# Cache tiles' outputs copied from input to output in memory instead of stored from SBUF

## The chip, the cores and the metric

The kernel runs on one core of a Trainium2 chip. The metric is the device time of one execution in microseconds. The engines named below are TensorE (PE; PEld is its weight load), VectorE (DVE), ScalarE (ACT), GpSimd (POOL) and SyncE (SP), which here issues nearly all of the DMA transfers. SBUF is the core's working memory, PSUM the memory that TensorE accumulates in; "memory" in this document is the chip's main memory, where inputs and outputs lie.

## The reference, cut to what matters

One layer of a decoder is computed for a prompt of 256 positions and for 8 sample sequences of 4 new positions each, all with the same weights. Besides the two activations the layer returns the caches of keys and values after the step. For the sample sequences that is the old cache with the new rows behind it:

```python
for g, (win, dil) in enumerate(GROUPS):
    kg, vg = k[:, :, g], v[:, :, g]
    ...
        kg = jnp.concatenate([kv_prev[g][:, :, 0].astype(x.dtype), kg], axis=1)
        vg = jnp.concatenate([kv_prev[g][:, :, 1].astype(x.dtype), vg], axis=1)
        o, l = _dilated_band_sample(q[:, :, g], kg, vg, slopes[g], dil)
    keep = min(win, kg.shape[1])
    kv_new.append(jnp.stack([kg[:, kg.shape[1] - keep:], vg[:, vg.shape[1] - keep:]], axis=2))
```

So the old rows of the three cache groups (windows 128, 512 and 2048) have to reach the outputs unchanged, and a part of them is also read by the attention of the sample sequences. In the third group, with its dilation of 16, attention reads 4 of 16 classes of rows; the other 12, called the rest, are only passed on. The rest of the layer is one input projection, a gated short convolution (mixer A), the attention (mixer B), two branch projections, an output projection, a layer norm, a feed-forward part with its own short convolution, and a second layer norm.

## The kernel before, in words

The host lays the arrays out by block. Weights lie as blocks of 128 x 2048 numbers (1 MB), one for each product. The part of the old cache that attention reads lies as 18 tiles of keys (`ck`) and 18 tiles of values (`cv`), 1 MB each: tiles 0 and 1 belong to the first group, 2 to 9 to the second, 10 to 17 to the third. The rest of the third group lies as 48 blocks of 1 MB (`rest`). The same layout holds for the outputs `o_ck`, `o_cv` and `o_rest`.

The kernel is a chain of 300 products on TensorE. Each multiplies one weight block with the 288 tokens in three passes of 16 matmuls (lines 222 to 224), for which a weight is split into a high part `whi` (by ScalarE) and a low part `wlo` (by VectorE), both in line 228, half a block at a time. The loaded block lies in `wst`, of which there are three buffers; `whi` and `wlo` have four buffers of half a block. `product` calls `prepare`, which issues the load of a later block on SP's queue (line 183), and then lets the steps of the sample attention run that are due (`sample_steps`). The order of the products is: queries, keys and values, then mixer A (48 products), gates and branch A in turns (32), gates and branch B in turns (32, branch B with blocks of 0.25 MB), the output projection (16), and three rounds of up and down projections.

The sample attention is a list of events with due times counted in products. A tile of the cache is loaded five products ahead of its work (`cache_load`, line 426, in one of three buffers `cache`), stored to its output three products ahead (`cache_store`, line 430), and then worked on. Tiles 0 and 1 are read by matmuls (line 476). All others are multiplied in place by queries or by attention weights: half of each half-tile by ScalarE (line 441), half by VectorE (line 445), and then summed by VectorE (line 447). Key tiles stand 2.75 products apart (`TILE_K`), value tiles 2.5 (`TILE_V`). A scheduler at build time puts the instructions of each engine in one order, by its own estimate of when each can run. The build also sets the waits, among them that of lines 441 and 445 for the store that reads the same tile, and that of the store for the load.

The rest of the third group goes from input to output in memory by `copy_rest` (line 147), one block behind every weight load number n with n above 116 and n modulo 11 equal to 0, 4 or 8 (line 187), which begins where branch B does. `behind` fixes an order on a queue without a wait. All of these transfers, weights, cache tiles, stores and copies, are issued by SP.

Of the kernel before, what the change touches and what calls it, by code (L numbers as in the profile page):

```python
# [20 lines left out]
KD = D // P  # L21
# [47 lines left out]
NB_QKV = 3 * NG * NH  # L69
N_CT = 18  # L70
N_REST = 48
# [22 lines left out]
def layer_kernel(ctx: ExitStack, tc: tile.TileContext, ins, outs):  # L94
    nc = tc.nc
    pe, dve, act, pool, sp = nc.tensor, nc.vector, nc.scalar, nc.gpsimd, nc.sync
# [12 lines left out]
    def sb(pl, shape, tag, dt=F32, bufs=None):  # L109
        return pl.tile(shape, dt, tag=tag, name=nm(tag), bufs=bufs)  # L110
# [22 lines left out]
    w_load = [None]  # L133
    steps_on = [False]
    n_product = [2]
    rest = [0]
    no_sync = mybir.DependencyInfo(mybir.DependencyClass.NoSync, mybir.DependencyReason.DATA)

    def behind(i, after):

        tc.add_manual_dep(i.ins, after.ins.name, no_sync, reason="pace")

    def copy_rest(after):
        if rest[0] < N_REST:
            n = rest[0]
            rest[0] += 1
            behind(sp.dma_start(outs["o_rest"][n], ins["rest"][n]), after)


    w_split = []  # L150
# [1 line left out]
    def half_block(st, k0, n):  # L152
        hi = sb(wp, [P, HK, P], "whi", F32R, bufs=4)
        lo = sb(wp, [P, HK, P], "wlo", F32R, bufs=4)
        w_split[:] = split(hi[:, :n, :], lo[:, :n, :], st[:, k0 : k0 + n, :])
        return hi, lo, n
# [21 lines left out]
    def prepare():  # L178
        src, nk = next(w_left, (None, 0))
        if nk == 0:  # L180
            return
        st = sb(wp, [P, KD, P], "wst")
        d = sp.dma_start(st[:, :nk, :], src.rearrange("p (k c) -> p k c", c=P))  # L183
        loads[0] += 1
        n = loads[0]
        w_load[0] = d
        if n > NB_QKV + 5 * KD and n % 11 in (0, 4, 8):
            copy_rest(d)
        w_ready.append([half_block(st, k0, min(HK, nk - k0)) for k0 in range(0, nk, HK)])

# [12 lines left out]
    def product(x):  # L203

        w = w_ready.pop(0)
        if not w_ready:
            prepare()
        n_product[0] += 1
        if steps_on[0]:
            next(steps, None)  # L210
        o = acc(x[0].shape[-1])
        mms(o, w, x)
        prompt_step()
        return o.rearrange("p a h -> p h a")
# [59 lines left out]
    def first_three():  # L274

        prepare()
        o = [acc() for _ in range(3)]

        def first_w(lo, b, k):
            if b < 2:  # L280
                return w_two_lo[k // HK][:, b, k % HK] if lo else w_two_hi[:, b, k]
            return (w_one_lo if lo else w_one_hi)[k // HK][:, k % HK]

        before = None
        for k0, n, _ in FIRST:
            for term in range(3):
                for k in range(k0, k0 + n):
                    xk = x[term == 1][:, k].rearrange("p h a -> p a h")
                    for b in range(3):
                        i = pe.matmul(  # L290
                            o[b], first_w(term == 2, b, k), xk, start=k == 0 and term == 0, stop=k == KD - 1 and term == 2
                        )
                        if before is not None:
                            behind(i, before)
                        before = i
        return [t.rearrange("p a h -> p h a") for t in o]
# [125 lines left out]
    cache_tiles = {}  # L422
# [3 lines left out]
        behind(sp.dma_start(t, ins[which][n]), w_load[0])  # L426
        cache_tiles[which, n] = t

    def cache_store(which, n):
        sp.dma_start(outs["o_" + which][n], cache_tiles[which, n])  # L430

    def weighted(which, n, half, w):

        c, (g, b) = cache_tiles[which, n], divmod(n - 2, NB)
        cols = NT * P
        for j in (2 * half, 2 * half + 1):
            e = c[:, j * cols : (j + 1) * cols]
            if j % 2 == 0:
                for t in range(NT):
                    e_t = e[:, t * P : (t + 1) * P]  # L440
                    act.activation(e_t, e_t, AF.Copy, scale=w[:, g + 1, j, b * NT + t : b * NT + t + 1])  # L441
            else:
                e3 = e.rearrange("p (t k) -> p t k", t=NT)
                w3 = w[:, g + 1, j, b * NT : (b + 1) * NT].unsqueeze(2).broadcast_to([P, NT, P])
                dve.tensor_tensor(e3, e3, w3, ALU.mult)  # L445
        j = slice(2 * half, 2 * half + 2)
        dve.tensor_reduce(  # L447
            parts[:, g, :, j, b * NT : (b + 1) * NT].rearrange("p k j t -> p j t k"),
            c[:, 2 * half * cols : (2 * half + 2) * cols].rearrange("p (j t k c) -> p j t k c", j=2, t=NT, c=SQ),
            AX.X, ALU.add, apply_transpose=True,  # L450
        )

    def sample_events():
# [98 lines left out]
        for which, w, first, apart in (("ck", q_s, SCORES_AT, TILE_K), ("cv", sT_w, VALUES_AT, TILE_V)):  # L552
            for n in range(N_CT):
                at = first + n if n < 2 else first + 2 + (n - 2) * apart
                yield at - 5, partial(cache_load, which, n)
                yield at - 3, partial(cache_store, which, n)
                if n < 2:
                    yield at - 1, partial(masks, n, w)
                    yield at, partial(first_group, which, n)
                else:  # L560
                    for half in range(2):
                        yield at + half * apart / 2, partial(weighted, which, n, half, w)

    events = sorted(sample_events(), key=lambda e: e[0])

    def sample_steps():
# [496 lines left out]
```

## Time and profile before

| | |
|---|---|
| median of 3 runs | 1748.38 us (1745.45 to 1749.07) |
| the profiled execution | 1746.45 us |
| its span, first to last instruction | 1744.7 us |
| mean granted TensorE clock | 0.995 |
| TensorE busy | 1717.8 us, 98% |
| VectorE, ScalarE, GpSimd busy | 1102.0, 866.2, 260.9 us |
| moved by DMA | 436.15 MB |
| read from memory, written to it | 389.78 MB, 94.53 MB |

A row of a group of instructions has its line, engine, operation, output and inputs by the program's names, shapes, count, busy time and mean duration. A row of waits has who waited, for whom, the sum in us, how often, and the longest. A row of DMA issues has the median time from issue to landing. In the rows of stretches each engine's busy time is followed by its number of instructions. A matmul's recorded end is modelled, and matmuls overlap, so that a busy TensorE need not be one at its full pace.

### The profile page before, as it was taken

To read this page: it belongs to the slowest core of one execution; us is meant where nothing else is said; L and a number is where in the kernel's file an instruction comes from. 1 tells how busy PE (TensorE), PEld (TensorE's weight loads), DVE (VectorE), ACT (ScalarE), POOL (GpSimd) and SP (SyncE) were. 2 spreads that over 40 slices of the span, in tenths; PEclk is the share of its full clock that TensorE was granted. 3 is DMA by queue.
4 is the path that set the end of the run, shared out by engine and by line. 5 is a ranking of instruction groups with operands and counts; after the bars stand their busy time and mean duration, and the time that the engine had idled before them with its cause. 6 is when DMAs were issued, how large, how long until landed. Compare 5 with 4: busy or idle time off the path is not lost.

```text
span 1744.7 us, 33546 instructions
## 1 busy us (share of the span) xinstructions
PE 1717.8 (98%) x14034; PEld 1710.6 (98%) x14034; DVE 1102.0 (63%) x1406; ACT 866.2 (50%) x1398; POOL 260.9 (15%) x404
## 2 busy tenths in 40 slices
PE   9999999999999999999999999999999999999996
PEld 9999999999999999999999999999999999999996
DVE  5566567666877664455688888865555554555554
ACT  5455465444556443344445655544445443344444
POOL 0000001100010000011264332300111100011165
PEclk9999999999999999999999999999999999999998
DMA  9886777877887874567766655656666565656662
GB/s 334 316 329 262 298 274 264 313 285 293 299 314 303 323 266 169 181 241 265 268 230 229 229 220 230 229 219 237 221 228 232 220 237 219 231 227 222 223 221 99
DMA packets 61496, 436.15 MB, mean 250 GB/s; under 512 B 7456, under 2 KB 9504, under 8 KB 17440
## 3 DMA queue, kind: packets, MB, share of 16 engines
q1 hardware_dynamic: 59616, 429.29, 65.6%
q10 hardware_dynamic: 1728, 4.72, 0.7%
q8 instruction: 109, 1.79, 0.4%
q14 instruction: 43, 0.35, 0.1%
HBM read 389.78 MB, written 94.53 MB: 278 GB/s over the span
## 4 chain that ended last, share of the span: by engine, by line
PE 78%; DMA 14%; DVE 3%; issue 2%; ACT 2%; SPq 0%; ACTq 0%; DVEq 0%; POOL 0%; POOLq 0%
PE acc L222 26%; PE acc L224 26%; PE acc L223 26%; DMA cache<-in_cv 4%; DMA cache<-in_ck 4%; DMA out_o_ck<-cache 4%; DMA out_o_cv<-cache 2%; DVE wlo L228 2%; ACT cache L441 1%; PE acc L290 1%; DVE sw L447 1%; DMA dd<-in_w_in 0%; SPq L183 0%; ACT whi L228 0%; ACT yah L789 0%
## 5 line engine op out<-in xcount | busy, mean ns | idle before, releaser
L228 DVE TENSOR_TENSOR wlo<-wst,whi 128x1024 fp32r<-128x1024 f32 (+2 forms) x584 | 704.0, 1211 | 415.3 <-ACT whi L228 413.5
L222 PE MATMUL acc<-xh,whi 128*128 128x288 f32 (+1 forms) x3216 | 922.1, 287 | 0.0
L224 PE MATMUL acc<-xh,wlo 128*128 128x288 f32 (+1 forms) x3216 | 917.9, 285 | 3.1 <-DVE wlo L228 3.0
L223 PE MATMUL acc<-xl,whi 128*128 128x288 f32 (+1 forms) x3216 | 919.6, 286 | 0.0
L228 ACT CAST whi<-wst 128x1024 fp32r<-128x1024 f32 (+2 forms) x584 | 588.8, 1015 | 642.4 <-PE acc L223 591.8
L224 PEld LDWEIGHTS acc<-xh,wlo 128*128 128x128 f32 x3216 | 605.4, 188 | 4.9 <-DVE wlo L228 4.8
L223 PEld LDWEIGHTS acc<-xl,whi 128*128 128x128 f32 x3216 | 606.8, 189 | 0.0
L222 PEld LDWEIGHTS acc<-xh,whi 128*128 128x128 f32 x3216 | 605.6, 188 | 1.0 <-issue 0.8
L224 PE MATMUL acc<-yah,wlo 128*128 128x288 f32 x1216 | 348.8, 287 | 1.9 <-DVE wlo L228 1.9
L222 PE MATMUL acc<-yah,whi 128*128 128x288 f32 x1216 | 348.4, 287 | 1.0 <-ACT whi L228 1.0
L223 PE MATMUL acc<-yal,whi 128*128 128x288 f32 x1216 | 348.5, 287 | 0.0
L224 PEld LDWEIGHTS acc<-yah,wlo 128*128 128x128 f32 x1216 | 230.5, 190 | 2.6 <-DVE wlo L228 2.6
L222 PEld LDWEIGHTS acc<-yah,whi 128*128 128x128 f32 x1216 | 230.4, 190 | 1.2 <-ACT whi L228 1.2
L223 PEld LDWEIGHTS acc<-yal,whi 128*128 128x128 f32 x1216 | 230.5, 190 | 0.0
L625 POOL COPY qk_s<-u 128x2 f32<-128x2 f32 x44 | 38.1, 865 | 572.1 <-ACT u L840 449.1
L447 DVE TRANSPOSE_TENSOR_REDUCE sw<-cache 128x32 f32<-128x1024 f32 x64 | 77.2, 1235 | 0.2
L613 DVE SCALAR_TENSOR_TENSOR cy<-u,prm,cy 128x304 f32<-128x304 f32 x120 | 73.5, 613 | 3.7 <-ACT cy L611 0.7
L441 ACT ACTIVATE cache<-cache,dd 128x128 f32<-128x128 f32 x128 | 39.6, 389 | 71.3 <-DMA out_o_cv<-cache 71.3
L441 ACT ACTIVATE cache<-cache,qk_s 128x128 f32<-128x128 f32 x128 | 39.7, 389 | 70.4 <-DMA out_o_ck<-cache 70.4
L445 DVE TENSOR_TENSOR cache<-cache,qk_s 128x512 f32<-128x512 f32 x32 | 20.8, 688 | 67.6 <-DMA out_o_ck<-cache 67.6
L685 POOL TENSOR_TENSOR ya<-ya,dd 128x288 f32<-128x288 f32 x16 | 13.6, 851 | 303.6 <-DVE ya L684 303.6
L445 DVE TENSOR_TENSOR cache<-cache,dd 128x512 f32<-128x512 f32 x32 | 20.8, 688 | 54.2 <-DMA out_o_cv<-cache 54.2
(181 smaller groups left out, 931.0 us busy)
## 6 DMA issues: line engine op xcount, KB each, us to landing
wst<-in_w_in SPq DMA_DIRECT2D x113, 1024.0 KB, 6.8
wst<-in_w_up SPq DMA_DIRECT2D x88, 1024.0 KB, 4.8
wst<-in_w_down SPq DMA_DIRECT2D x32, 1024.0 KB, 4.8
cache<-in_ck SPq DMA_DIRECT2D x18, 1024.0 KB, 8.0
out_o_ck<-cache SPq DMA_DIRECT2D x18, 1024.0 KB, 6.5
cache<-in_cv SPq DMA_DIRECT2D x18, 1024.0 KB, 8.3
out_o_cv<-cache SPq DMA_DIRECT2D x18, 1024.0 KB, 6.7
wst<-in_w_a SPq DMA_DIRECT2D x16, 1024.0 KB, 5.1
```

The source lines that it names most:

```text
L222: pe.matmul(out, hi[:, c, :], xh_k, start=k == 0, stop=False)
L223: pe.matmul(out, hi[:, c, :], xl_k, start=False, stop=False)
L224: last_mm[0] = pe.matmul(out, lo[:, c, :], xh_k, start=False, stop=k == nk - 1)
L228: return act.copy(hi, src), dve.tensor_tensor(lo, src, f32(hi), ALU.subtract)
L290: i = pe.matmul(o[b], first_w(term == 2, b, k), xk, start=k == 0 and term == 0, stop=k == KD - 1 and term == 2)
L441: act.activation(e_t, e_t, AF.Copy, scale=w[:, g + 1, j, b * NT + t : b * NT + t + 1])
L445: dve.tensor_tensor(e3, e3, w3, ALU.mult)
L447: dve.tensor_reduce(parts[:, g, :, j, b * NT : (b + 1) * NT].rearrange("p k j t -> p j t k"), c[:, 2 * half * cols : (2 * half + 2) * cols ...
L613: dve.scalar_tensor_tensor(y, u[:, i : i + YW], prm[:, w0 + i : w0 + i + 1], y, ALU.mult, ALU.add)
L625: pool.tensor_copy(dst[:, 0:2], u[:, SEQ : SEQ + 2])
L685: pool.tensor_tensor(m, m, ma[:, i], ALU.add)
```

## The change

The 36 stores of cache tiles and their events go. The outputs `o_ck` and `o_cv` are written by copies from the inputs `ck` and `cv`, in memory, which stand in one list with the 48 blocks of the rest. The list is taken from its end: value tiles first, then key tiles, then the rest. A copy now stands behind every weight load number n with n above 92 and n modulo 7 equal to 0, 2 or 4. The due times of the cache loads and of the work on the tiles stay as they are. Line numbers of the changed kernel are lower by one from line 148 on and by up to five further down.

```diff
-    rest = [0]
+    rest = [("o_rest", "rest", n) for n in range(N_REST)] + [("o_" + c, c, n) for c in ("ck", "cv") for n in range(N_CT)]
...
     def copy_rest(after):
-        if rest[0] < N_REST:
-            n = rest[0]
-            rest[0] += 1
-            behind(sp.dma_start(outs["o_rest"][n], ins["rest"][n]), after)
+        if rest:
+            dst, src, n = rest.pop()
+            behind(sp.dma_start(outs[dst][n], ins[src][n]), after)
...
-        if n > NB_QKV + 5 * KD and n % 11 in (0, 4, 8):
+        if n > NB_QKV + 3 * KD + 8 and n % 7 in (0, 2, 4):
             copy_rest(d)
...
-    def cache_store(which, n):
-        sp.dma_start(outs["o_" + which][n], cache_tiles[which, n])
-
...
                 yield at - 5, partial(cache_load, which, n)
-                yield at - 3, partial(cache_store, which, n)
```

## The prediction

> **What bounds the kernel now.** I read the page first (TensorE busy nearly throughout), then the span cut into stretches, then the waits.
>
> ```profile
> 150.00:250.00 100.00, 96.45 (x764) 95.15 (x764) 62.06 (x88) 52.78 (x105) 2.86 (x6) 0.98 0.75 284
> 250.00:450.00 200.00, 199.92 (x1702) 198.62 (x1701) 136.77 (x194) 103.50 (x183) 20.73 (x44) 1.00 0.76 287
> 450.00:600.00 150.00, 147.48 (x1191) 146.13 (x1190) 106.87 (x132) 81.08 (x152) 7.12 (x20) 1.00 0.81 313
> 600.00:650.00 50.00, 47.15 (x367) 46.50 (x366) 29.96 (x32) 23.11 (x43) 0.00 (x0) 0.97 0.75 282
> 650.00:1700.00 1050.00, 1050.00 (x8564) 1049.68 (x8564) 655.50 (x821) 504.72 (x746) 199.99 (x295) 1.00 0.61 226
> ```
>
> The columns are length, then busy time and count of PE, PEld, DVE, ACT, POOL, then TensorE's granted clock, the DMA share and GB/s. From 650 to 1700 us TensorE never pauses: 8564 matmuls in 1050 us, one per 122.6 ns, so a product of 48 matmuls takes 5.89 us. No removed wait can save anything there. What TensorE loses lies between 150 and 650 us, where the cache tiles are worked on: 3.55 + 0.08 + 2.52 + 2.85 = 9.0 us idle. The waits of TensorE from 100 to 650 us name who was late:
>
> ```profile
> PE acc L224 <- DVE wlo L228: 4.9, 8, 1.2
> PE att L356 <- ACT dd L593: 2.6, 1, 2.6
> PE acc L222 <- ACT whi L228: 1.0, 1, 1.0
> PE acc L388 <- DVE yal L374: 0.3, 1, 0.3
> ```
>
> These are 11 waits for VectorE and ScalarE. The page says why those two were late, and what their queue neighbour SP did:
>
> ```profile
> ACT cache L441 <- DMA out_o_cv<-cache: 71.3, 15, 7.9
> ACT cache L441 <- DMA out_o_ck<-cache: 70.4, 16, 9.2
> ...
> SPq L183 <- DVE wlo L228: 1217.3, 255, 13.4
> SPq L430 <- DMA cache<-in_ck: 65.2, 16, 6.4
> SPq L430 <- DMA cache<-in_cv: 60.8, 17, 9.5
> ```
>
> The tiles are scaled in place, so L441 and L445 must wait until the store has read the tile: 141.7 us on ScalarE, 4.6 us a tile. SP first waits for the load to land (126 us, about 4 us a tile) before it can issue that store, with weight loads queued behind.
>
> **What can be won at most.** 9.0 us idle. The clock rows 0.98 x 100 us and 0.97 x 50 us cost 2.0 + 1.5 = 3.5 us; both follow the longest pauses. A matmul is recorded at 287 ns but the next starts after 122.6, so each of the 11 pauses hides another 0.165 us: 1.8 us. Together 14.3 us, by stretch: 150 to 250 about 6.0, 450 to 600 about 3.5, 600 to 650 about 4.8. The lower end of the span is set by this: 1746.45 - 14.3 = 1732.
>
> **The change, part by part.**
>
> *36 stores and their waits go.* Released is the wait, but the work behind it does not simply slide forward: the new build keeps the order on SP (less the stores, plus the copies), TensorE and GpSimd, and moves the scaling of a tile ahead of two to four weight splits (wlo, whi) on VectorE and ScalarE. These splits now stand behind the landing of the load, where before they ran while it was under way. One tile of each stretch shows what that leaves.
>
> Tile nine of ck (counted from zero), the chain of waits, then ScalarE's timeline:
>
> ```profile
> 187.94 6.93 DMA cache<-in_ck
> 194.89 4.81 DMA out_o_ck<-cache
> ```
>
> ```profile
> 199.78 0.40 ACT L441 ACTIVATE cache<-cache,qk_s 128x128 f32<-128x128 f32 x1 [9.17 <-DMA out_o_ck<-cache]
> 200.09 1.03 ACT L228 CAST whi<-wst 128x1024 fp32r<-128x1024 f32 x1
> 201.03 0.40 ACT L441 ACTIVATE cache<-cache,qk_s 128x128 f32<-128x128 f32 x1
> 201.33 0.38 ACT L593 COPY dd<-acc 128x288 f32<-128x288 f32 x1
> ```
>
> TensorE waited 2.6 us for that L593, so it was ready near 199.1. After: landed at 194.87, eight L441 at 0.3 us, two casts at 1.0, then L593 ends near 199.7. 2.6 us become 0.6, and a pause that short should not cost the clock. With the smaller pauses of this stretch (0.8 to 1.3 us) cut similarly, I leave 1.5 of 6.0 us. Bounds: 0, and the 6.0 of now.
>
> Tile fifteen of ck stands for the convolution stage: the chain, then VectorE.
>
> ```profile
> 299.28 7.75 DMA cache<-in_ck
> 307.05 4.93 DMA out_o_ck<-cache
> ```
>
> ```profile
> 302.51 1.22 DVE L228 TENSOR_TENSOR wlo<-wst,whi 128x1024 fp32r<-128x1024 f32 x1
> 303.64 0.52 DVE L636 TENSOR_TENSOR ya<-cy,acc 128x256 f32<-128x256 f32 x2
> 304.08 1.21 DVE L228 TENSOR_TENSOR wlo<-wst,whi 128x1024 fp32r<-128x1024 f32 x1
> 305.21 0.45 DVE L228 TENSOR_TENSOR yal<-ya,yah 128x288 fp32r<-128x288 f32 x1
> 305.88 1.23 DVE L228 TENSOR_TENSOR wlo<-wst,whi 128x1024 fp32r<-128x1024 f32 x1 [0.21 <-ACT whi L228]
> 312.07 1.29 DVE L445 TENSOR_TENSOR cache<-cache,qk_s 128x512 f32<-128x512 f32 x2 [4.96 <-DMA out_o_ck<-cache]
> 313.37 2.42 DVE L447 TRANSPOSE_TENSOR_REDUCE sw<-cache 128x32 f32<-128x1024 f32 x2
> 315.71 2.31 DVE L228 TENSOR_TENSOR wlo<-wst,whi 128x1024 fp32r<-128x1024 f32 x2
> ```
>
> The next cache load follows a weight load that the first split of the last row releases, at 317.30:
>
> ```profile
> 317.30 0.42 SPq L426 DMA_DIRECT2D cache<-in_ck  x1
> ```
>
> So a tile costs 18.02 us, against three products, 17.65 us: the loop is what paces this stage, by a hair. Without the store, 4.93 us leave it, but three splits, ya and yal move behind the load: 1.3 + 2.4 + four splits of 1.2 + 0.5 + 0.45 = 9.4 us. With 0.4 us on SP: 7.75 + 9.4 + 0.4 = 17.5 us; with a load of 6.93 us as in the tile above, 16.7. Most of the 4.93 us is given back, yet the loop falls under TensorE's 17.65. Cv tiles come 2.5 products apart, in pairs: two loads at 7.4 with their issue, two tiles' work at 3.7, and, by the new order, five of ten splits and about 1.1 us of the rest outside a load's shadow: 14.8 + 7.4 + 6 + 1.1 = 29.3 against five products, 29.4. No slack builds up, so I leave 1.5 of the 3.5 us. Bounds: 0, and for a load 1 us longer (2 - 0.1) x 8 pairs = 15 us.
>
> *36 copies come, with denser pacing.* They hang behind weight loads number 93 onwards, three in seven, where 48 hung three in eleven from 117. Load 297 is the last; the places up to it number 88 for 84 copies, and the 84th stands at load 287, where the 48th stood at 290: the tail is not touched. The first ones meet the last three cv loads, each now queued right behind a copy. A transfer behind a weight load lands some 2.2 us later than a load alone (7.0 for a copy against 4.8, rows below), and a load behind both later again. Two to four us more for those loads eat most of what the store leaves; of the 4.8 us in 600 to 650 I leave 3.0. Bounds: 0, and 4.8 + 3 x 2 = 11.
>
> The other copies fall where TensorE never pauses:
>
> ```profile
> wst<-in_w_down SPq DMA_DIRECT2D x32, 1024.0 KB, 4.8
> cache<-in_ck SPq DMA_DIRECT2D x18, 1024.0 KB, 8.0
> out_o_ck<-cache SPq DMA_DIRECT2D x18, 1024.0 KB, 6.5
> cache<-in_cv SPq DMA_DIRECT2D x18, 1024.0 KB, 8.3
> ...
> out_o_rest<-in_rest SPq DMA_DIRECT2D x48, 7.0
> ```
>
> ```profile
> 735.00:835.00 100.00, 100.00 (x817) 100.00 (x816) 55.92 (x67) 45.86 (x66) 10.37 (x13) 1.00 0.69 256
> 789.00:795.00 6.00, 6.00 (x51) 6.00 (x50) 3.40 (x4) 2.59 (x5) 0.62 (x1) 1.00 0.96 369
> ```
>
> A load's buffer comes round every three products, 17.65 us. Landing takes 4.8, the second half's split waits half a product (2.9) and both splits take some 2.2: 7.7 us are spare, and SP's 255 waits for a free buffer say the same. A copy ahead of a load can add at most its own 7.0. Never do two copies follow each other. Worst is the w_b stretch (735 to 845 us), a pair of products in 1.25 x 5.89 = 7.36 us: today's copies do stand ahead of loads there and TensorE is busy 100.00 of 100 us; some five more, each 2.7 us of all engines (1.05 MB at 369 / 0.96 GB/s), raise the share from 0.69 to about 0.83. I take 0 us. Without that cover it is 5 x (7.0 - 4.8) = 11 us.
>
> **Sum.** 14.3 - (1.5 + 1.5 + 3.0) = 8.3 us, against the profiled execution's 1746.45 us (span 1744.7, 1.75 around it): 1738. That execution is 1.9 us under the median, 1748.38, and inside the three runs (1745.45 to 1749.07), so I forecast 1738 and let the range carry the 1.9. A change under 0.2%, 3.5 us, can hardly be told from none here.
>
> **Rivals.**
> *All pauses go*: loads without stores beside them land so early that even the moved splits are ahead. For it: SP no longer stands 4 us a tile. Against: 17.5 of 17.65 us. 1732.
> *The wait only changes its name*: L441 and L445 wait for the load as long as for the store, and the splits behind pay it all. For it: 9.4 us now stand behind the load. 1746.
> *The loop becomes the bound*, slower: one mechanism, the cache load's time from issue to landing. From 7.85 us (17.65 - 9.4 - 0.4) every tile is late. At 9 us some 28 tiles lose 1.15 us each, 32 in all, in place of the 14.3 lost now: 1746.45 - 14.3 + 32 = 1764. For it: the medians of 8.0 and 8.3. Against: those contain loads behind stores.
> *The memory takes no more*, slower: GB/s above counts a copied byte once, memory moves it twice. Now 256 GB/s and 7.4 copies of 1.05 MB in 100 us, 78 GB/s, make 334. After, a pair of w_b products needs 1.31 MB of loads and 6/7 of a copy's 2.1, 3.1 MB. At no more than 334 GB/s it takes 9.3 instead of 7.36 us, over 16 pairs 31, less 7.7 spare: 1738 + 23 = 1761. Against: from 789 to 795 us 369 GB/s with a copy inside run at 369 + 1.05 MB / 6 us = 544. [...]
> That the change doesn't do what it says is excluded by the counts: 84 copies in 88 places, no store left.
>
> **How the numbers follow.** Forecast 0.56 (own range 1733 to 1743), all pauses gone 0.10, wait renamed 0.16, loop bound 0.12, memory 0.04, anything else slower 0.02. Faster 0.66, same 0.16, slower 0.18. The range goes from the floor of 1732, less 1, to 1750: over the renamed wait with the median's 1.9, and a few us into the loop bound.
>
> **What would show it.** Right: L441 and L445 wait for cache<-in_ck and in_cv, 2 to 5 us at about half the tiles; TensorE's idle time between 150 and 600 us falls under 3 us; the clock rows there read 1.00; a pause or two stay between 600 and 650; cache loads land in about 7 us; 650 to 1700 us stays at 100%, the DMA share there near 0.68. Wrong: cache loads at 8 us or more with TensorE waiting for wlo at every tile, or any wait of ScalarE for wst behind a copy with TensorE idle after 735 us.

## The result and the profile after

| | before | after |
|---|---|---|
| median of 4 runs, us | 1748.59 | 1737.93 |
| lowest to highest, us | 1745.45 to 1749.07 | 1737.08 to 1739.33 |
| span of the profiled execution, us | 1744.7 | 1736.0 |

The ratio is 0.9944 with a 95% interval of 0.9926 to 0.9961: the change makes the kernel faster by 10.7 us, and the forecast was 1738. The runs of before are the three named above and a fourth. In the three later sets of runs the median of before is 1746.3 to 1747.0 us, so some 2 of the 10.7 us lie within the spread of before; the spans of the two profiled executions differ by 8.7 us. Line numbers below are those of each kernel: L441, L445, L447, L426 and L183 of before are L437, L441, L443, L425 and L182 after. The experiments e1, e2, e4, e5 and e8 are edits of before and have its lines; e3, e6, e7 and e9 are edits of after.

The same stretches of the changed kernel, and the w_b stretch behind them (length; busy time and count of PE, PEld, DVE, ACT, POOL; clock; DMA share; GB/s):

```profile
150.00:250.00 100.00, 99.50 (x810) 98.98 (x809) 66.33 (x95) 56.12 (x109) 3.13 (x6) 1.00 0.62 230
250.00:450.00 200.00, 200.00 (x1708) 199.13 (x1707) 138.45 (x194) 104.07 (x182) 6.94 (x44) 1.00 0.62 234
450.00:600.00 150.00, 146.67 (x1183) 145.17 (x1182) 103.18 (x127) 81.59 (x150) 5.05 (x20) 1.00 0.62 240
600.00:650.00 50.00, 48.91 (x393) 48.12 (x392) 30.78 (x32) 22.31 (x37) 0.00 (x0) 1.00 0.82 319
650.00:1700.00 1050.00, 1050.00 (x8564) 1049.68 (x8564) 656.11 (x823) 505.75 (x749) 204.15 (x301) 1.00 0.68 257
735.00:835.00 100.00, 100.00 (x817) 100.00 (x816) 56.64 (x69) 47.24 (x68) 11.15 (x14) 1.00 0.82 306
```

Two things are to be read here. The clock is 1.00 everywhere. And the counts of matmuls say more than the busy time. The modelled end of a matmul (285 to 287 ns in the mean, where the next one starts after 122.6) hides a part of each pause, and the lower clock in before left TensorE busy but slower (0.50 from 625.39 us on: 16 matmuls in 3.41 us, busy throughout); both show as matmuls that a stretch of fixed length doesn't hold. Against before, 150 to 250 holds 46 more (810 against 764), 250 to 450 6 more, 450 to 600 8 fewer, and 600 to 650 26 more: 70 matmuls at 122.6 ns are 8.6 us, and the spans differ by 8.7. From 650 us on both hold 8564. So the gain is all in the tile stages, where it was looked for, but the stretch 450 to 600 lost a little.

Waits of the changed kernel (who, for whom; us in total, times, longest):

```profile
ACT cache L437 <- DMA cache<-in_cv: 58.3, 15, 8.3
...
DVE cache L441 <- DMA cache<-in_cv: 52.3, 14, 6.5
...
ACT cache L437 <- DMA cache<-in_ck: 21.4, 12, 6.0
```

ScalarE now waits for the load itself: 79.7 us in 27 waits, where it waited 141.7 us in 31 for the stores. SP no longer waits for the landing of a cache tile (126.0 us before). TensorE's waits from 100 to 650 us:

```profile
PE acc L223 <- DVE wlo L227: 3.7, 6, 1.2
PE acc L387 <- DVE yal L373: 0.5, 1, 0.5
PE acc L221 <- ACT whi L227: 0.5, 2, 0.3
```

The pause of 2.6 us for `dd` is gone; six short ones for `wlo` stay. Who made those late is in the chain of waits of the changed kernel (start us, us, what), among its longest pieces:

```profile
519.50 8.81 DMA cache<-in_cv
...
552.50 8.28 DMA cache<-in_cv
...
567.39 8.17 DMA cache<-in_cv
...
598.30 10.30 DMA cache<-in_cv
...
616.92 9.98 DMA cache<-in_cv
```

Five of the last seven value loads stand on the chain with 8 to 10 us each, and none is followed by a store. From 519.50 to 552.50 us, two tiles or five products, 33.0 us pass, where TensorE needs 29.4 (five times 5.89). The DMA issues of the page (median us to landing last):

```profile
wst<-in_w_in SPq DMA_DIRECT2D x113, 1024.0 KB, 4.9
...
cache<-in_ck SPq DMA_DIRECT2D x18, 1024.0 KB, 7.2
cache<-in_cv SPq DMA_DIRECT2D x18, 1024.0 KB, 8.0
...
out_o_rest<-in_rest SPq DMA_DIRECT2D x48, 7.0
```

Weight loads of the first stages land 1.9 us sooner than before (6.8), key tiles 0.8, value tiles only 0.3.

### The profile page after: what moved, and what is told of

Its sections match the earlier page's. It is cut to its first block, busy times and chain, and to the rows that moved or that the text cites. A ratio compares the mean times of both kernels' runs of the same rounds, so it can differ in the third digit from the quotient of the medians.

```text
span 1736.0 us, 33482 instructions
## 1 busy us (share of the span) xinstructions
PE 1714.2 (99%) x14034; PEld 1708.0 (98%) x14034; DVE 1103.5 (64%) x1406; ACT 869.6 (50%) x1398; POOL 244.3 (14%) x404
## 2 busy tenths in 40 slices
DMA packets 57463, 436.14 MB, mean 251 GB/s; under 512 B 7456, under 2 KB 9504, under 8 KB 17440
## 3 DMA queue, kind: packets, MB, share of 16 engines
HBM read 427.53 MB, written 94.53 MB: 301 GB/s over the span
## 4 chain that ended last, share of the span: by engine, by line
PE 92%; DMA 4%; DVE 2%; ACT 1%; issue 1%; SPq 0%; ACTq 0%; DVEq 0%
PE acc L221 30%; PE acc L223 30%; PE acc L222 30%; DMA cache<-in_cv 3%; PE acc L289 1%; DVE wlo L227 1%; DMA cache<-in_ck 1%; DVE sw L443 1%; PE att L395 0%; DMA wst<-in_w_in 0%; ACT cache L437 0%; ACT whi L227 0%; ACT yah L784 0%; DVE dd L760 0%; PE att L472 0%
## 5 line engine op out<-in xcount | busy, mean ns | idle before, releaser
L443 DVE TRANSPOSE_TENSOR_REDUCE sw<-cache 128x32 f32<-128x1024 f32 x64 | 77.3, 1232 | 0.4 <-ACT cache L437 0.3
L437 ACT ACTIVATE cache<-cache,dd 128x128 f32<-128x128 f32 x128 | 39.3, 388 | 58.3 <-DMA cache<-in_cv 58.3
L441 DVE TENSOR_TENSOR cache<-cache,dd 128x512 f32<-128x512 f32 x32 | 20.8, 688 | 52.3 <-DMA cache<-in_cv 52.3
L437 ACT ACTIVATE cache<-cache,qk_s 128x128 f32<-128x128 f32 x128 | 39.6, 389 | 22.5 <-DMA cache<-in_ck 21.4
L227 ACT CAST yah<-ya 128x288 fp32r<-128x288 f32 x76 | 32.7, 430 | 24.7 <-DVE ya L631 8.5
```

What stands on the lines that cost most here:

```text
L227: return act.copy(hi, src), dve.tensor_tensor(lo, src, f32(hi), ALU.subtract)
L443: dve.tensor_reduce(parts[:, g, :, j, b * NT : (b + 1) * NT].rearrange("p k j t -> p j t k"), c[:, 2 * half * cols : (2 * half + 2) * cols ...
```

## The experiments

The theory: what was gained is the dependence on the store (the work in place waits until the store has read the tile, and the store until the load has landed). Rivals: the traffic beside the loads (36 stores of 1 MB), or SP's queue standing at the store with weight loads behind it. A second question is what the copies cost, a third what is left in 450 to 600. Each ratio is to runs of before on the same chip: their median is 1747.0 us for e1, e2, e4 and e5, 1746.26 for e3, e6, e7 and e8, and 1746.42 for e9.

The table gives the matmuls of each stretch, from rows like those above. It accounts for the spans: e9's 1728.6 us, plus 122.6 ns for each matmul that a kernel has fewer than e9, comes within 0.3 us of the kernel's span. The exceptions are e1, off by 1.0 us, and e4; both also lost matmuls outside these stretches.

| kernel | 150-250 | 250-450 | 450-600 | 600-650 | span | median us | ratio (95%) |
|---|---|---|---|---|---|---|---|
| before | 764 | 1702 | 1191 | 367 | 1744.7 | 1748.59 | |
| after | 810 | 1708 | 1183 | 393 | 1736.0 | 1737.93 | 0.9944 (0.9926 to 0.9961) |
| e1 no store | 811 | 1707 | 1171 | 407 | 1736.6 | 1737.16 | 0.9945 (0.993 to 0.996) |
| e2 rest copies denser | 769 | 1695 | 1205 | 403 | 1738.8 | 1743.41 | 0.9982 (0.9971 to 0.9993) |
| e3 copies late | 815 | 1708 | 1175 | 410 | 1734.3 | 1735.71 | 0.9939 (0.9923 to 0.9956) |
| e4 stores by GpSimd | 815 | 1581 | 1110 | 349 | 1776.2 | 1777.14 | 1.0184 (1.016 to 1.0207) |
| e5 copy in the store's place | 815 | 1675 | 1212 | 403 | 1734.7 | 1737.56 | 0.9945 (0.993 to 0.996) |
| e6 loads earlier | 815 | 1707 | 1215 | 410 | 1729.4 | 1730.76 | 0.991 (0.989 to 0.993) |
| e7 work later | 811 | 1707 | 1179 | 389 | 1737.1 | 1738.44 | 0.9953 (0.9935 to 0.997) |
| e8 before, loads and stores earlier | 796 | 1657 | 1188 | 387 | 1743.9 | 1745.82 | 0.9992 (0.9976 to 1.0008) |
| e9 e3 and e6 | 816 | 1708 | 1219 | 410 | 1728.6 | 1730.83 | 0.9909 (0.9893 to 0.9926) |

### e1: the stores alone go

```diff
-                yield at - 3, partial(cache_store, which, n)
```

> The kernel before without the 36 stores; the old cache rows of the tiles are not written at all (o_ck and o_cv are left out), the 48 copies of the rest stay as before. Wait theory (the work on a tile stood behind its store): all of the gain is here, 1736 to 1738 us, TensorE idle 5 to 7 us between 150 and 650 us less what the copies cost beside the last value loads (about 1.5 us). Queue theory (SP stood for the landing of loads, so weights came late) and traffic theory (the stores' bytes made loads late) expect the same here; this run prices the copies: if the changed kernel is slower than this one by more than 2 us, the copies cost that.

1737.16 us, the ratio of the changed kernel. This kernel writes the old rows of the tiles nowhere. The whole gain comes with the stores' going; the 36 copies and their denser places take nothing from it that could be measured. Its stretches, 450 to 650:

```profile
450.00:600.00 150.00, 145.59 (x1171) 143.87 (x1170) 102.40 (x126) 80.76 (x150) 5.21 (x20) 1.00 0.60 232
600.00:650.00 50.00, 49.85 (x407) 49.63 (x406) 31.73 (x33) 23.65 (x38) 0.00 (x0) 1.00 0.63 240
```

The loss in 450 to 600 is there though this kernel's first copy goes out at 727 us, so the copies aren't its cause. In 600 to 650 it holds 14 matmuls, 1.7 us, more than the changed kernel, whose first copies go out from 583 us on; in the stretch before it holds 12 fewer, and why is not known.

### e5: a copy in the place of each store

```diff
-        sp.dma_start(outs["o_" + which][n], cache_tiles[which, n])
+        behind(sp.dma_start(outs["o_" + which][n], ins[which][n]), w_load[0])
```

> The kernel before with each store replaced, at its own place in SP's queue and with its own due time, by a copy of the same tile from input to output in memory: the same bytes at the same time, but nothing waits for the tile's landing and no work on a tile waits for the copy. Wait and queue theory: most of the gain stays, 1738 to 1742 us, cache loads landing in about 8.5 us. Traffic theory: no gain, 1746 to 1750 us.

The same bytes are written at the same places in SP's queue, but nothing waits for them and they wait for no load: 1737.56 us, the same ratio again. The loads land in 9.2 and 8.3 us (ck, cv), key tiles later than before (8.0) and value tiles the same, and ScalarE waits for them:

```profile
ACT cache L441 <- DMA cache<-in_cv: 71.6, 14, 6.8
...
ACT cache L441 <- DMA cache<-in_ck: 52.1, 13, 6.8
```

123.7 us, against 141.7 before, and yet the gain is all there. Traffic as the cause falls. It also shows how little ScalarE's sum of waits says: what counts is whether the splits behind are late for TensorE. The gain lies elsewhere than in the changed kernel: 250 to 450 lacks 33 matmuls against e9 and 450 to 600 only 7, where the changed kernel lacks none and 36.

### e4: the stores on GpSimd's queue

```diff
-        sp.dma_start(outs["o_" + which][n], cache_tiles[which, n])
+        pool.dma_start(outs["o_" + which][n], cache_tiles[which, n])
```

> The kernel before with the stores issued from GpSimd's queue instead of SP's: SP no longer stands for the landing of a load, but the work on a tile still waits for its store. Wait theory: ScalarE and VectorE still wait 100 us or more each for the stores, 1744 to 1752 us. Queue theory: weights come in time and the gain is here, 1738 to 1741 us. GpSimd has other work in that stretch that now stands behind the stores' wait, which can add some us.

1777.14 us, slower by 1.8%. SP waits for no landing any more, but GpSimd does, and the work still waits for the store. Two of its waits, then pieces of the chain of waits from 584 us on:

```profile
POOL out_o_cv L430 <- DMA cache<-in_cv: 187.8, 18, 21.9
...
ACT cache L441 <- DMA out_o_cv<-cache: 64.5, 11, 10.8
```

```profile
584.21 7.15 DMA cache<-in_cv
591.41 0.51 issue
591.91 10.41 DMA out_o_cv<-cache
...
602.95 0.14 DVE cache L445
603.10 0.46 issue
603.55 1.23 DVE wlo L228
604.83 0.61 PE acc L224
605.44 0.24 PE acc L222
...
611.04 0.12 PE acc L222
```

Load, store, work, split, matmul, one behind the other: 18.1 us from the load's issue until the store has landed and the tile may be scaled. Freeing SP alone gains nothing, so SP's queue is not needed to explain the loss. The trace of before says the same: from 150 to 650 us its list of ScalarE's waits names none for a weight block (`wst`), and by the records a block landed 6.1 us ahead of its split in the median and less than 1 us ahead only twice. The run doesn't give the price of SP's wait by itself, as these stores are slower too (7.3 and 8.0 us to landing in the median, 6.5 and 6.7 from SP) and GpSimd's other work stands behind its own waits. A kernel with SP's wait and without the work's wait wasn't tried.

### e8: before, with loads and stores two products earlier

```diff
-                yield at - 5, partial(cache_load, which, n)
-                yield at - 3, partial(cache_store, which, n)
+                yield at - 7, partial(cache_load, which, n)
+                yield at - 5, partial(cache_store, which, n)
```

> The kernel before, stores and all, with loads due seven and stores due five products ahead of the work instead of five and three. If the store hurts only because it is late when the work comes: the waits for stores fall below 40 us on each engine and the time is 1733 to 1738 us, the whole gain of the change without the change. If the order on SP or the bytes of the store are what costs: 1744 us or more.

No gain: 0.9992, the interval holds 1. ScalarE's waits for the stores fell by a quarter, to 107 us, and not under the 40 us that the expectation asked for; TensorE's longest pause is 3.5 us, where it was 2.6:

```profile
ACT cache L441 <- DMA out_o_cv<-cache: 56.2, 13, 7.6
ACT cache L441 <- DMA out_o_ck<-cache: 51.2, 14, 6.4
...
PE att L396 <- ACT yah L392: 5.2, 2, 3.5
```

The same two products make 6 to 7 us without the store (e6, below). With the store, going earlier didn't take the wait away: load and store moved forward, and most of the wait stayed. So the run doesn't say what a store would cost that is done in time.

### e2: the rest's copies at the new density, stores as before

```diff
-        if n > NB_QKV + 5 * KD and n % 11 in (0, 4, 8):
+        if n > NB_QKV + 3 * KD + 8 and n % 7 in (0, 2, 4):
```

> The kernel before with only the pacing of the changed one: the 48 blocks of the rest behind weight loads from 93 on, three in seven, so that the first copies stand beside the last value loads and stores. If copies there cost what the prediction put on them (loads 2 to 4 us later): TensorE idle between 600 and 650 us grows from 2.9 to 5 us or more and the time is 1750 to 1754 us. If copies beside loads are free: 1748 us, as before.

A miss: 1743.41 us, 0.2% faster than before instead of slower. Below are the stretch that was to suffer, the longest of TensorE's waits from 100 to 650 us, and the stretch in which that wait lies:

```profile
600.00:650.00 50.00, 49.32 (x403) 49.11 (x402) 32.07 (x33) 24.59 (x45) 0.00 (x0) 1.00 0.98 382
```

```profile
PE att L356 <- ACT dd L593: 2.9, 1, 2.9
```

```profile
150.00:250.00 100.00, 95.59 (x769) 94.22 (x768) 62.46 (x89) 53.09 (x106) 2.86 (x6) 1.00 0.75 284
```

The DMA engines are busy 0.98 of the time beside the last value loads, stores and copies, and TensorE idles 0.7 us there, not 2.85 as before. The loads did get later: the last three took 10.3 to 14.1 us, in before 7.9 to 9.4. So the copies made these loads later, but the later loads cost TensorE no more than those 0.7 us. The pause for `dd` is as in before and a little longer (2.9 against 2.6 us), but the clock stays at 1.00. Why before's two pauses of 1.0 and 1.2 us, at 622 to 625 us, don't come here isn't settled. The medians differ by 3.6 us, with 10 runs of this kernel.

### e3: the copies begin later

```diff
-        if n > NB_QKV + 3 * KD + 8 and n % 7 in (0, 2, 4):
+        if n > NB_QKV + 5 * KD and n % 2 == 0:
```

> The changed kernel with its 84 copies behind every second weight load from 118 on, so that none stands beside a cache load but the stretch of branch B and all later ones carry more. Prediction's step on the last value loads: TensorE's idle 1.1 us at 600 to 650 us goes to 0.2 or less, 1736 to 1737.5 us. If a half of all loads with a copy behind is too much for branch B (735 to 845 us): TensorE idles there and the time is 1739 to 1750 us.

1735.71 us; some 2 us under the changed kernel, with intervals that overlap widely. 600 to 650 holds 410 matmuls without a pause, against 393, or 2.1 us; 450 to 600 holds 8 fewer than the changed kernel, so over both stretches the copies beside the last three value loads cost 1.1 us. And every second weight load behind 116 can carry a copy:

```profile
650.00:1700.00 1050.00, 1050.00 (x8564) 1049.68 (x8564) 657.90 (x824) 505.76 (x749) 203.80 (x301) 1.00 0.70 262
```

### e6: the loads two products earlier

```diff
-                yield at - 5, partial(cache_load, which, n)
+                yield at - 7, partial(cache_load, which, n)
```

> The changed kernel with every cache tile loaded seven instead of five products ahead of its work; the three buffers are free some 30 us before the loads go out, so nothing should hold them. Loop theory (what is left of TensorE's pauses at 500 to 650 us is the work waiting for a load that lands 7 to 10 us after its issue): the waits of ScalarE and VectorE for cache loads go from 80 and 69 us to under 20 each, TensorE idles under 1 us between 150 and 650 us, 1732 to 1734 us. Rival: the scheduler moves the work forward by as much, the wait stays, 1737 to 1739 us.

1730.76 us, 0.991: another 6 to 7 us (5.9 by the ratios, 6.6 by the spans, 7.2 by the medians), and faster than both kernels. Its stretches from 450, and TensorE's waits from 100 to 650:

```profile
450.00:600.00 150.00, 149.06 (x1215) 148.84 (x1214) 107.04 (x131) 82.99 (x152) 4.95 (x20) 1.00 0.67 259
600.00:650.00 50.00, 50.00 (x410) 50.00 (x409) 26.53 (x27) 21.14 (x30) 0.00 (x0) 1.00 0.75 290
```

```profile
PE acc L223 <- DVE wlo L227: 0.9, 1, 0.9
```

Half of the expectation missed: ScalarE still waits 65.5 us for the loads (79.7 after) and not under 20, so the work moved forward with them, as the rival said; but the time fell below the range given for the first theory. What changed is the pace. The value loads on SP from 440 to 600 us, first in the changed kernel, then here (issue ns, first and last start; next line us to landing min/median/max):

```profile
L425 SPq DMA_DIRECT2D cache<-in_cv x11: 423/427/1324, 442.6 to 598.3; - x11
...
DMA to landing us min/median/max: 6.9/8.3/10.9
```

```profile
L425 SPq DMA_DIRECT2D cache<-in_cv x11: 419/427/1392, 447.8 to 598.7; - x11
...
DMA to landing us min/median/max: 6.8/7.0/10.5
```

Ten steps take 155.7 us after and 150.9 here, but they aren't the same tiles: the seventh to the seventeenth value load after, the eighth to the eighteenth here. From the seventh to the seventeenth this kernel takes 147.5 us (433.9 to 581.4). So the changed kernel spends 15.57 us a tile and this one 14.75 on the same tiles, against TensorE's 14.72 (2.5 x 5.89). The changed kernel drifts by 0.85 us a tile. By the instruction records the split `wlo`, which is ready some 6.7 us ahead of its matmul where nothing presses, is ready 0.06 us ahead at nine places from 534 us on; here it comes that close twice. The stage also begins about two products earlier. How much of the gain belongs to the pace and how much to the earlier start wasn't separated.

### e7: the work on a tile 0.75 products later

```diff
-                        yield at + half * apart / 2, partial(weighted, which, n, half, w)
+                        yield at + 0.75 + half * apart / 2, partial(weighted, which, n, half, w)
```

> The changed kernel with the work on a tile due 0.75 product later and the loads where they are, so that fewer weight splits stand behind a load's landing. If the two to four splits that the new order moved behind the landing are what gives part of the gain back: waits for cache loads fall by half or more and the time is 1733 to 1736 us. If not: 1737 to 1739 us.

1738.44 us, 0.9953 (0.9935 to 0.997): no difference from the changed kernel, and its waits for loads are nearly the same (53.2 and 22.0 us on ScalarE, 58.3 and 21.4 in the changed kernel). The due time of the work alone does not decide where it runs; the experiment says nothing about what later work would give.

### e9: loads earlier and copies late

e3 and e6 in one.

> The changed kernel with both edits that gave something alone: the cache loads are due seven work items ahead of their tile in place of four, and the 48 copies of the third group's rest begin only behind the fifth stretch of weight loads, on every second of them. Theory (what was left of the pauses after the change came from loads that land too close to the split that reads them, and from nothing else of weight): with the early loads TensorE idled 0.94 us in 450 to 600 and had one pause of 0.9 us at 596, beside value loads that shared the DMA engines with copies; with no copy there that pause goes too, idle 150 to 650 is under 0.5 us, and the time is 1729.5 to 1731. Rival (the late copies gave their 2 us for another reason, by leaving the stretch 600 to 735 alone): that adds to the early loads, and the time is 1728 to 1729.5. Rival (the two edits gain the same pauses and the w_b stretch, with its DMA share near 0.9, has no cover left when all copies stand later): 1731 to 1734, with waits of the w_b splits for their loads and idle of TensorE behind 735.

(Five, not four, is the lead that seven replaces, and all 84 copies come late, not 48.) 1730.83 us, the same as e6 with 1730.76: the first theory. The 2 us of e3 don't add: the earlier loads had already taken those pauses away.

```profile
450.00:600.00 150.00, 149.50 (x1219) 149.29 (x1218) 107.36 (x131) 83.95 (x152) 5.50 (x20) 1.00 0.63 248
600.00:650.00 50.00, 50.00 (x410) 50.00 (x409) 26.05 (x27) 21.16 (x29) 0.00 (x0) 1.00 0.55 209
```

TensorE idles 0.5 us between 150 and 650. What is left for this kernel lies outside the tile stages.

## Why the prediction was right, point by point

**The cause** was right and is shown: no store, or a copy in the store's very place, gives the ratio of the whole change (e1, e5), and stores on another queue don't (e4). That SP's wait made no weights late is read from the trace of before; what it does to the cache loads was not separated.

**What can be won at most**, 14.3 us, was too small. e9 has a span of 1728.6: before lost 16.1 us against it, and the stretches lack 52, 6, 28 and 43 matmuls, 6.4 + 0.7 + 3.4 + 5.3 us, against the 6.0, 0, 3.5 and 4.8 of the prediction. Counting the matmuls that each stretch lacks would have given this without adding up idle time, clock and hidden ends. So the floor of 1732 was 1 us above what e6 and e9 reach.

**150 to 250, 1.5 us left:** 6 matmuls, 0.7 us. The pause of 2.6 us for `dd` went altogether, where 0.6 us of it was to stay; one of 0.5 us, for `yal`, is left. The clock is at 1.00 with it, as it was in before from 450 to 600 us with five pauses of up to 0.7 us.

**The key tiles of the convolution stage, 17.5 against 17.65 us:** they kept pace. The last three loads stand 17.7 us apart, and TensorE idled 0 us from 250 to 450. As before idled only 0.08 us there, this tests the sum little; the clearer sign is that ScalarE's waits for ck loads are short, 1.8 us each.

**The value tiles, 29.3 against 29.4 us and 1.5 us left:** this is the step that failed. A pair took 31.1 us (2 x 15.57), and 36 matmuls, 4.4 us, are missing in 450 to 600 against e9, more than the 28 of before. The term that was mis-sized is the load: 7.0 us without its issue were put in, and the ten loads of these steps took 8.2 in the mean. That makes 16.4 in place of 14.0 us a pair; all the rest of the pair took 14.7, in place of 15.3, although 6.4 splits `wlo` a pair began behind a landing and not the five that were put in. The stores' going did not quicken the stage at all: in before the same ten steps took 15.35 us a tile.

A long load alone doesn't make the stage late. In e5 the loads of these tiles took 8.7 us, and yet the tiles come 14.96 us apart, as only 12.6 us of a pair lie outside the loads (12.4 in before). The records show where the difference lies: of the 49 to 51 splits `wlo` of these ten steps, 30 began while a load was under way in before, 26 in e5 and 17 in the changed kernel. So the order of the build counts as much as the load; no run moved the splits alone. The order on SP in the changed kernel:

```profile
519.12 0.33 SPq L182 DMA_DIRECT2D wst<-in_w_a  x1
519.50 0.43 SPq L425 DMA_DIRECT2D cache<-in_cv  x1
521.90 0.33 SPq L182 DMA_DIRECT2D wst<-in_w_in  x1
```

The cache load goes out 0.38 us behind a weight load, and a second weight load follows 2.4 us later, while it is under way: this is the load of 8.81 us on the chain. That its two neighbours cost it the 1 to 2 us over the shortest of the eleven (6.9 to landing) is an estimate from the trace, not tested. The prediction's own price for this case, 15 us, was too high, as it let every pair be late at once. By the records the lead of the splits, up to 6.7 us, was used up first.

**The first copies beside the last value loads, 2 to 4 us more for each:** right. These loads took 10.9, 10.3 and 10.0 us to landing, and in e3, with no copy near them, 8.5, 6.9 and 7.0: 2.4 to 3.4 us more. Left in 600 to 650 were 17 matmuls, 2.1 us, predicted 3.0. In e3 none is left there.

**The other copies, 0 us:** right. The w_b stretch has a share of 0.82 (0.83 was predicted) and no pause.

So 7.2 us were left in place of 6.0, out of 15.8 in place of 14.3: a gain of 8.6 in place of 8.3, where two errors of more than 1 us cancel. In three of the four stretches the size was off by 0.8 to 2.9 us; only the sum was near. That the median came within 0.1 us of the forecast is luck.

**The rivals.** The renamed wait is there in the rows (79.7 us for loads), but TensorE lacks no more than 4.4 us in the stretch where it is longest. The loop as the bound came true in the value stage alone, where the same 4.4 us are what it cost, and not 32. That all pauses go needed the loads earlier (e6). That the memory takes no more falls: the w_b stretch of the changed kernel moved 306 GB/s for 100 us with TensorE never idle, and the issues of that stretch are

```profile
out_o_cv<-in_cv SPq DMA_DIRECT2D x6, 7.0
out_o_ck<-in_ck SPq DMA_DIRECT2D x5, 6.9
```

11 copies of 1.05 MB whose bytes memory moves twice, so another 115 GB/s: 421 in all, where the rival allowed no more than 334. The pages show the second move: with 36 copies in place of the stores, reads from memory go from 389.78 to 427.53 MB (36 x 1.05), while writes stay at 94.53 MB and what DMA moved at 436.15 and 436.14.

**What would show it:** the waits came under the names foreseen, 3.9 us each for value tiles and 1.8 for key tiles; the clock rows and the 0.68 behind 650 us came as said. Idle time from 150 to 600 was 3.8 us, not under 3, and loads of value tiles took 8.0 us, not 7: both are the failed step. So the sign for a wrong prediction came in part: loads at 8 us, but TensorE waited for `wlo` at six places and not at every tile.

## What to carry to other kernels

A store that reads a tile which is then overwritten in place puts the landing of the load, the issue and the whole store ahead of the work (18.1 us in e4's chain); where the bytes are only passed on, a copy in memory takes both waits away, and here its own traffic cost nothing that could be measured (0.9945 with it in e5, 0.9945 without it in e1). When a wait goes, look for the next one in the same place, here the load (79.7 us on ScalarE): see at once whether it can go out earlier, as long as its buffer is free; here that was worth 6 to 7 us more for one number. When a wait goes, check too what the build moves behind the next one: here splits that used to run during the load went behind its landing (17 in place of 30 began during one), and the value stage gained nothing. And count the matmuls in a stretch instead of adding up pauses.

## What was not expected of the hardware

Not every pause cost the clock here, and those of before that did were shorter than one of e2 that didn't. Before shows 0.98 over 150 to 250 us: by the records the clock was 0.50 for 3.41 us, from 202.14 us on, behind the pause of 2.6 us that ended at 201.76. The second drop, of the same length, began at 625.39 us, behind two pauses of 1.0 and 1.2 us. e2 had the pause for `dd` with 2.9 us at 1.00. What a drop costs shows in before, where the second one holds 16 matmuls and 3.41 us at 122.6 ns would hold 28, and in e4's chain (clock 0.93 over 600 to 650 us): matmuls 0.24 us apart behind 604.83, 0.12 again from 611 on. Why a pause of 2.6 us cost the clock and one of 2.9 us didn't, no run here shows. 13 runs of before on one chip lie from 1742.45 to 1750.31 us, the four of e6 from 1730.15 to 1731.24; whether drops of the clock make up that spread is not shown.

The DMA engines took a share of 0.98 for 50 us (e2, 382 GB/s beside copies) without a pause of TensorE of more than 1 us. The loads there did land later, at up to 14.1 us, but here a share of 0.98 by itself was no sign that TensorE would stand still.
